# A hybrid decoder layer on one core: in the state-space stage the product is made in place in `yv`, its square goes into the spent `xt` tile, and ScalarE's queue stores it

## The chip, the cores and the metric

The kernel runs on one core of one Trainium2 chip. A core has TensorE (PE in the profile, with its weight loads as PEld), VectorE (DVE), ScalarE (ACT), GpSimd (POOL) and SyncE (SP). Each engine works through its own list of instructions in order; an instruction that has to wait holds up everything behind it on that engine. Transfers between main memory and on-chip memory are issued by an engine's sequencer (SPq, ACTq, POOLq in the profile), on that engine's queue and in that engine's order. The metric is the time of one execution in microseconds (us) on the device; lower is better.

## The reference, cut to what matters

One layer of a decoder trunk with 512 tokens and a width of 1024: RMSNorm, one wide projection `h @ W_in`, three token mixers side by side (top-k attention "DSA", block-sparse attention "NSA", a state-space mixer "SSD"), a gated sum, an output projection, and a feed-forward part. All is float32. The change lies in the end of the state-space mixer:

```python
def ssd_mixer(z, xbc, dt, ...):          # 4 groups x 4 chunks of 128 tokens, 8 heads of 64 per group
    xbc = silu(causal_conv(xbc, conv_w, conv_b))
    ...
    y_diag = einsum('bcijg,bcijgh,bcjgh,bcjghp->bcighp', cb, lmat, dtc, xs)
    states = einsum('bcjgn,bcjgh,bcjghp->bcghpn', bm, decay_states * dtc, xs)
    ...                                   # the state is carried from chunk to chunk
    y_off = einsum('bcign,bcghpn,bcigh->bcighp', cm, h_in, exp(a_cum))
    y = y_diag + y_off + xs * d_skip
    y = rms_norm(y * silu(z), norm_g)     # needs y * silu(z) and the sum of its squares per token
    return y
```

## The kernel before, in words

Two streams of work are interleaved on the engines. The **filler** is the large projections: weights are loaded by SP into `wraw` (3 buffers, L154), split by ScalarE (`whi`, L173) and VectorE (`wlo`, L175) into two parts, and multiplied on TensorE in three passes (L459, L460, L461). The **main** stream is the mixers, stage by stage. A `yield` in the main stream hands over a number of nanoseconds, and the filler is advanced by as much; so the text of the program interleaves both. The framework's scheduler then puts the instructions of each engine in an order of its own, from what waits for what, from the buffers and from priorities; a change in one place can therefore move instructions in the whole of a stage and in those behind it.

The state-space stage has 16 units (group g, chunk c), two groups alternating. Unit i runs through three steps. `stage1` issues the loads of `bcx` (3 buffers) and `E` (3 buffers, 512 KB) on SP. `load_xz` issues the loads of `xs` (2 buffers, L1330) and `xz` (3 buffers, 512 KB, L1332) on SP; half of `xz` is the skip term `u.xd`, the other half the gate `u.zs`. `stage2` masks `E` (POOL, L1345), takes exponentials (ACT: `eab` L1344, `E` L1348), makes `xt` and `xw` on POOL (2 buffers each; L1350, L1353) and multiplies `E` by a small product in bank `pv` (DVE, L1355). `stage3` makes up to two accumulators of tag `sc` (2 banks) and the state update (`hst`, L1374, L1377), eight products per unit of `xt` with `E` on TensorE (L1315), and then the end that the change touches:

- L1384, VectorE: `yv` = product + (`t1`, which lies in `eab`, or the skip term). `yv` has **one** buffer.
- L1395, VectorE: `zs` = `yv` times `zs`, written **into the gate's half of the `xz` tile**.
- L1396, SP: store of that half into `yc_d`, 256 KB. Until it has landed, this buffer of `xz` can't be loaded again.
- L1397, ScalarE: square of `zs` into `yv`.
- L1401, L1403, L1404, POOL: the halves of the square are added, and added to the sums `sq` of that chunk. Until then `yv` can't be written again.

The last two units take another branch (L1386 to L1394): the pool `tl` is open by then, with `zsl` (2 buffers) for the product and `sk` for the sums on VectorE. The outputs `yc_d` are read back much later, in the branch projections (L825).

Of the kernel before, what the change touches and what calls it, by code (L numbers as in the profile page):

```python
# [7 lines left out]
F32 = mybir.dt.float32  # L8
F32R = mybir.dt.float32r
AF = mybir.ActivationFunctionType  # L10
ALU = mybir.AluOpType
# [30 lines left out]
def build_kernel(ctx, tc, A, out):  # L42
    nc = tc.nc
    pe, act, dve, pool = nc.tensor, nc.scalar, nc.vector, nc.gpsimd
# [5 lines left out]
    def bc(ap, shape):  # L50
        return ap.to_broadcast(shape)
# [6 lines left out]
    def popen(name, side="left", space=None, bufs=1):  # L58
        kw = dict(name=name, bufs=bufs, side=side)
        if space is not None:  # L60
            kw["space"] = space
            kw.pop("side")
        cm = tc.tile_pool(**kw)
        p = cm.__enter__()
        open_pools[name] = cm
        return p
# [6 lines left out]
    def scratch(name, shape, dt=F32):  # L73
        return scr_pool.tile(shape, dt, name=name)
# [8 lines left out]
    yc_d = scratch("yc_d", [4, NB, 128, 512])  # L83
# [8 lines left out]
    def ps(tag, shape, dt=F32, bufs=2):  # L92
        if tag == XT[0]:
            XT[1] += 1
            if XT[1] % 3 == 0:
                tag = "pF"
        return psp.tile(shape, dt, tag=tag, name=tag, bufs=PSB[tag])
# [1209 lines left out]
    def ssd(sv, ratio):  # L1307
        sp = popen("ssd", side="right")
# [5 lines left out]
        def mm(*a):  # L1314
            i_ = pe.matmul(*a, start=True, stop=True)  # L1315
            tc.stamp_issue_order_token(getattr(i_, "ins", i_), "ssd")
# [41 lines left out]
        def stage3(u):  # L1358
            g, c = u.g, u.c
            py = ps("sc", [128, 512])  # L1360
            if c:
                po = ps("sc", [128, 512])
                for k in range(4):
                    mm(po[:, 128 * k:128 * k + 128], hst[g][:, 128 * k:128 * k + 128], u.b[:, 1])
                t1 = u.ea.rearrange("p k i -> p (k i)")
                dve.tensor_tensor(t1, po, t1, op=ALU.mult)
                pool.tensor_tensor(t1, t1, u.xd, op=ALU.add)
                yield ratio * 960
            if c < 3:
                pst = ps("pT", [128, 512])  # L1370
                mm(pst, u.b[:, 2], u.xw)
                if c == 0:
                    hst[g] = sp.tile([128, 512], F32, name="hst", bufs=2)
                    act.activation(hst[g], pst, AF.Copy)  # L1374
                else:
                    pool.tensor_tensor(x3(hst[g]), x3(hst[g]), bc(col(sv["dec"], c, g)[:, :, None], [128, 8, 64]), op=ALU.mult)
                    dve.tensor_tensor(hst[g], hst[g], pst, op=ALU.add)  # L1377
                yield ratio * 858
            for h in range(8):
                e, cs = h % 2, slice(128 * (h // 2), 128 * (h // 2) + 128)  # L1380
                mm(py[64 * e:64 * e + 64, cs], u.xt[:, h * 64:h * 64 + 64], u.E[:, h])
            yield ratio * 1300
            yv = (TL[0] or sp).tile([128, 512], F32, name="yv", bufs=1)
            dve.tensor_tensor(yv, py, t1 if c else u.xd, op=ALU.add)  # L1384
            if TL[0] is not None:
                zs = TL[0].tile([128, 512], F32, name="zsl", bufs=2)  # L1386
                dve.tensor_tensor(zs, yv, u.zs, op=ALU.mult)
                nc.sync.dma_start(yc_d[g, c], zs)
                act.activation(yv, zs, AF.Square)
                dve.tensor_tensor(yv[:, 0:256], yv[:, 0:256], yv[:, 256:512], op=ALU.add)  # L1390
                for k in range(2):
                    dve.tensor_tensor(SK[:, c], SK[:, c], yv[:, 128 * k:128 * k + 128], op=ALU.add)
                yield ratio * 100
                return  # L1394
            dve.tensor_tensor(u.zs, yv, u.zs, op=ALU.mult)  # L1395
            nc.sync.dma_start(yc_d[g, c], u.zs)  # L1396
            act.activation(yv, u.zs, AF.Square)  # L1397
            lo, hi = yv[:, 0:256], yv[:, 256:512]
            if sq4[c] is None:
                sq4[c] = sp.tile([128, 256], F32, name=f"sq{c}")  # L1400
                pool.tensor_tensor(sq4[c], lo, hi, op=ALU.add)  # L1401
            else:
                pool.tensor_tensor(lo, lo, hi, op=ALU.add)  # L1403
                pool.tensor_tensor(sq4[c], sq4[c], lo, op=ALU.add)  # L1404
            yield ratio * 100
# [16 lines left out]
        TL, SK = [None], None  # L1422
        for i in range(16):
            if i == 14:
                yield "nq"
                TL[0] = popen("tl")
                SK = TL[0].tile([128, NB, 128], F32, name="sk")
                for c in range(NB):
                    dve.tensor_tensor(SK[:, c], sq4[c][:, 0:128], sq4[c][:, 128:256], op=ALU.add)
            yield from need(i + 2)  # L1430
            if i + 2 < 16:
                load_xz(us[i + 2])
            if i + 1 < 16:
                yield from stage2(us[i + 1])
            yield from stage3(us[i])
# [444 lines left out]
```

## Time and profile before

| | |
|---|---|
| median of 3 runs | 1348.6 us (1346.11 to 1349.12) |
| the profiled execution | 1348.39 us, of which the span of the profile is 1346.7 us |
| PE busy | 1327.0 us, 99% of the span |
| DVE, ACT, POOL busy | 997.3, 728.3, 272.7 us |
| moved by the DMA queues | 213.74 MB, nearly all issued by SP (q1) |
| state-space stage | some 165 us, from the first loads at 405 us to the last product at 566 us |

How to read it: a row of the timeline has its start and its duration in us, the engine, the line, the tiles written and read, and in square brackets how long the engine was idle before it and what ended that. A row of the waits has the engine and the line that waited, what it waited for, the total in us, how often, and the longest. In the table by windows the first column after the stretch is its length, and then the busy time of each engine; "DMA share" is the mean busy share of the 16 DMA engines. Matmuls overlap, so idle time of PE is time in which none was in flight.

### The profile page before, as it was taken

What the parts mean: (1) busy time and instruction counts of PE and PEld (TensorE: products, weight loads), DVE (VectorE), ACT (ScalarE), POOL (GpSimd) and SP (SyncE); (2) the same over time, 40 slices, a digit from 0 to 9 for tenths busy, and PEclk for the clock granted to TensorE, in tenths of its full rate; (3) what the DMA queues carried; (4) which work ended last, traced back from release to release, by engine and by line L of the source; (5) the groups of instructions that cost most, each with busy time, mean ns of one, the idle gap of its engine ahead of it and who ended that gap; (6) DMA issues with size and microseconds to landing.
All of it is one profiled execution on the core that took longest, in us unless ns stands there. A gap on an engine that the chain in (4) does not pass through costs nothing.

```text
span 1346.7 us, 19637 instructions
## 1 busy us (share of the span) xinstructions
PE 1327.0 (99%) x6827; PEld 1107.3 (82%) x6827; DVE 997.3 (74%) x1977; ACT 728.3 (54%) x1395; POOL 272.7 (20%) x238
## 2 busy tenths in 40 slices
PE   9999999999999999999999999999999999999998
PEld 7788888888887767788888888888889888888887
DVE  6489986889977657667688789988654666757841
ACT  5456334777767764656676666565343443444520
POOL 2325111111005669500000022222000201102000
PEclk8999999999999999999999999999999999999999
DMA  6336665455459889653354546343527646746431
GB/s 199 112 91 160 186 180 135 131 158 145 142 160 325 288 283 313 214 175 103 108 155 125 162 133 175 118 149 124 175 78 188 132 151 140 169 124 128 148 121 47
DMA packets 251777, 213.74 MB, mean 159 GB/s; under 512 B 15881, under 2 KB 203165, under 8 KB 251678
## 3 DMA queue, kind: packets, MB, share of 16 engines
q1 hardware_dynamic: 235708, 188.88, 46.4%
q0 software_dynamic: 15232, 20.98, 8.2%
q10 hardware_dynamic: 738, 2.63, 0.6%
q8 instruction: 54, 0.88, 0.3%
q14 instruction: 45, 0.37, 0.1%
HBM read 171.75 MB, written 40.70 MB: 158 GB/s over the span
## 4 chain that ended last, share of the span: by engine, by line
PE 86%; DVE 4%; DMA 4%; POOL 2%; issue 2%; ACT 1%; SPq 0%; DVEq 0%; ACTq 0%; POOLq 0%
PE pj L459 20%; PE pj L461 20%; PE pj L460 20%; PE sc L459 4%; PE sc L460 4%; PE sc L461 3%; PE pT L987 3%; PE pv L999 2%; PE pv L1000 2%; PE sc L928 2%; PE sc L927 2%; PE sc L1315 1%; DMA xs<-x_d 1%; PE pF L987 1%; DMA q_d<-qev 1%
## 5 line engine op out<-in xcount | busy, mean ns | idle before, releaser
L173 ACT ACTIVATE whi<-wraw 128x1024 fp32r<-128x1024 f32 (+2 forms) x190 | 198.3, 1046 | 239.0 <-PE pj L460 117.2
L175 DVE TENSOR_TENSOR wlo<-wraw,whi 128x1024 fp32r<-128x1024 f32 (+1 forms) x176 | 224.7, 1278 | 99.1 <-ACT whi L173 96.4
L459 PE MATMUL pj<-hTh,whi 128*128 128x512 f32 x512 | 203.3, 397 | 3.6 <-DVE cacc L856 2.0
L461 PE MATMUL pj<-hTh,wlo 128*128 128x512 f32 x512 | 202.1, 395 | 0.0
L460 PE MATMUL pj<-hTl,whi 128*128 128x512 f32 x512 | 202.0, 395 | 0.0
L936 ACT ACTIVATE p<-p,nb,rs 128x384 f32<-128x384 f32 (+3 forms) x160 | 107.8, 677 | 37.2 <-DVE nb L934 36.9
L459 PEld LDWEIGHTS pj<-hTh,whi 128*128 128x128 f32 x512 | 96.3, 188 | 22.8 <-ACT eab L1344 2.2
L460 PEld LDWEIGHTS pj<-hTl,whi 128*128 128x128 f32 x512 | 96.3, 188 | 19.1 <-issue 0.7
L461 PEld LDWEIGHTS pj<-hTh,wlo 128*128 128x128 f32 x512 | 96.2, 188 | 19.0 <-issue 0.4
L460 PE MATMUL pj<-h2l,whi 128*128 128x512 f32 (+1 forms) x256 | 96.3, 376 | 0.0
L461 PE MATMUL pj<-h2h,wlo 128*128 128x512 f32 (+1 forms) x256 | 96.2, 376 | 0.0
L459 PE MATMUL pj<-h2h,whi 128*128 128x512 f32 (+1 forms) x256 | 96.1, 376 | 0.0
L459 PE MATMUL pj<-whi,hTh 128*128 128x512 f32 (+2 forms) x208 | 81.3, 391 | 3.0 <-DVE v_s L561 2.2
L460 PE MATMUL pj<-wlo,hTh 128*128 128x512 f32 (+2 forms) x208 | 81.0, 390 | 0.0
L461 PE MATMUL pj<-whi,hTl 128*128 128x512 f32 (+2 forms) x208 | 80.5, 387 | 0.0
L991 ACT ACTIVATE pth<-pT 128x512 fp32r<-128x512 f32 x92 | 53.1, 593 | 48.0 <-PE pT L987 47.5
L1046 POOL DMA_DIRECT2D qu<-q_d x32 | 23.5, 737 | 263.5 <-PE sc L928 175.3
L992 DVE TENSOR_TENSOR ptl<-pT,pth 128x512 fp32r<-128x512 f32 x92 | 61.9, 680 | 5.1 <-ACT pth L991 5.0
L459 PE MATMUL sc<-whi,fh 128*128 128x512 f32 x168 | 65.4, 389 | 0.0
L460 PE MATMUL sc<-wlo,fh 128*128 128x512 f32 x168 | 65.4, 389 | 0.0
L461 PE MATMUL sc<-whi,fo 128*128 128x512 f32 x168 | 65.2, 389 | 0.0
L987 PE MATMUL pT<-ident,p 128*128 128x128 f32 x368 | 60.2, 272 | 0.5 <-DVE p L973 0.5
(431 smaller groups left out, 3281.5 us busy)
## 6 DMA issues: line engine op xcount, KB each, us to landing
wraw<-in_w_in_dram SPq DMA_DIRECT2D x84, 512.0 KB, 4.0
wraw<-in_w_ff_dram SPq DMA_DIRECT2D x58, 512.0 KB, 4.1
qd<-in_w_ff_dram POOLq DMA_DIRECT2D x18, 512.0 KB, 5.8
gld<-g_d SPq DMA_DIRECT2D x35, 256.0 KB, 2.8
q_d<-qev SPq DMA_DIRECT2D x64, 128.0 KB, 4.5
qu<-q_d POOLq DMA_DIRECT2D x32, 256.0 KB, 4.1
E<-ac_d SPq DMA_DIRECT2D x16, 512.0 KB, 6.7
xz<-xzt_d SPq DMA_DIRECT2D x16, 512.0 KB, 5.6
```

The source lines that it names most:

```text
L173: act.activation(hi[:, :m], r[:, :m], AF.Copy)
L175: (pool if i in LOWP else dve).tensor_tensor(lo[:, :m], r[:, :m], f(hi[:, :m]), op=ALU.subtract)
L459: pe.matmul(o, lh, rh, start=first, stop=False)
L460: pe.matmul(o, lh, rl, start=False, stop=False)
L461: pe.matmul(o, ll, rh, start=False, stop=last)
L927: pe.matmul(s_[:, h % w, :n], u.q[h], kh[:, :n], start=True, stop=False)
L928: pe.matmul(s_[:, h % w, :n], u.q[h], kl[:, :n], start=False, stop=True)
L936: act.activation(u.p[h][:, :n], u.p[h][:, :n], AF.Exp, bias=u.nb[:, h:h + 1], scale=rs8[:, u.b, u.h0 + h:u.h0 + h + 1], accum_out=u.sm[:, ...
L987: pe.transpose(pt[:, h], u.p[h][:, kb * 128:kb * 128 + 128], ident)
L991: act.activation(ph, ptf, AF.Copy)
L992: dve.tensor_tensor(pl, ptf, f(ph), op=ALU.subtract)
L999: pe.matmul(o, vk, ph0, start=st, stop=False)
```

## The change

In all units the product is written in place into `yv`. The square goes into `u.xt`, whose data the eight products have read by then (in the last two units into a tile `sqx` of its own, and `yv` has two buffers there). The store is issued by ScalarE, behind the square, and reads `yv`. So a buffer of `xz` is free when the product has been made, `yv` is free when the square and the store have read it, and a buffer of `xt` is free when POOL has added the squares.

```diff
-            yv = (TL[0] or sp).tile([128, 512], F32, name="yv", bufs=1)
+            yv = (TL[0] or sp).tile([128, 512], F32, name="yv", bufs=1 if TL[0] is None else 2)
             dve.tensor_tensor(yv, py, t1 if c else u.xd, op=ALU.add)
+            dve.tensor_tensor(yv, yv, u.zs, op=ALU.mult)
+            s2 = u.xt if TL[0] is None else TL[0].tile([128, 512], F32, name="sqx", bufs=2)
+            act.activation(s2, yv, AF.Square)
+            act.dma_start(yc_d[g, c], yv)
             if TL[0] is not None:
-                zs = TL[0].tile([128, 512], F32, name="zsl", bufs=2)
-                dve.tensor_tensor(zs, yv, u.zs, op=ALU.mult)
-                nc.sync.dma_start(yc_d[g, c], zs)
-                act.activation(yv, zs, AF.Square)
-                dve.tensor_tensor(yv[:, 0:256], yv[:, 0:256], yv[:, 256:512], op=ALU.add)
+                dve.tensor_tensor(s2[:, 0:256], s2[:, 0:256], s2[:, 256:512], op=ALU.add)
                 for k in range(2):
-                    dve.tensor_tensor(SK[:, c], SK[:, c], yv[:, 128 * k:128 * k + 128], op=ALU.add)
+                    dve.tensor_tensor(SK[:, c], SK[:, c], s2[:, 128 * k:128 * k + 128], op=ALU.add)
                 yield ratio * 100
                 return
-            dve.tensor_tensor(u.zs, yv, u.zs, op=ALU.mult)
-            nc.sync.dma_start(yc_d[g, c], u.zs)
-            act.activation(yv, u.zs, AF.Square)
-            lo, hi = yv[:, 0:256], yv[:, 256:512]
+            lo, hi = s2[:, 0:256], s2[:, 256:512]
```

The scheduler's order moves with it, on all engines, from the first unit's end on and through the NSA stage. Three places, around the change from the first pair of groups to the second (about 479 to 505 us of the profile before). First SP, whose list holds the loads of the later units; `q_d` are stores of the query projection. Before:

```order
L1396 DMA yc_d<-xz 128x512
L627 DMA q_d_2_67<-qev 64x512 x4
L1332 DMA xz<-xzt_d 128x2x512
L1323 DMA bcx<-bct_d 128x3x128
L1325 DMA E<-ac_d 128x1024
L1330 DMA xs<-x_d 128x512
```

Now:

```order
L627 DMA q_d_2_67<-qev 64x512 x4
L1332 DMA xz<-xzt_d 128x2x512
L1323 DMA bcx<-bct_d 128x3x128
L1325 DMA E<-ac_d 128x1024
L627 DMA q_d_3_68<-qev 64x512
L1330 DMA xs<-x_d 128x512
```

The store of `yc_d` ahead of them has gone from SP's list; the load of `xz`, with `bcx` and `E` behind it, stands where it stood.

ScalarE, at the same place (`hst` is the copy of a new group's first state). Before:

```order
L622 ACTIVATE qev<-pF 128x512
L1344 ACTIVATE eab<-E 64x512 x2
L1374 ACTIVATE hst<-pT 128x512
L1397 ACTIVATE yv<-xz 128x512
L1348 ACTIVATE E<-E,sv_nac 128x128 x8
```

Now:

```order
L622 ACTIVATE qev<-pF 128x512
L1344 ACTIVATE eab<-E 64x512 x2
L1387 ACTIVATE xt<-yv 128x512
L1388 DMA yc_d<-yv 128x512
L1374 ACTIVATE hst<-pT 128x512
L610 ACTIVATE qraw<-pj 128x512
L612 ACTIVATE sq<-qraw 128x512
L1348 ACTIVATE E<-E,sv_nac 128x128 x8
```

The square is now ahead of `hst`, and the issue of the store stands right behind it; both still stand behind `eab`, which waits for `E`.

VectorE, at the same place. Before:

```order
L1384 TENSOR_TENSOR yv<-sc,eab 128x512
L1355 TENSOR_TENSOR E<-E,pv 128x1024
L1395 TENSOR_TENSOR xz<-yv,xz 128x512
L1384 TENSOR_TENSOR yv<-sc,xz 128x512
L1355 TENSOR_TENSOR E<-E,pv 128x1024
```

Now:

```order
L1384 TENSOR_TENSOR yv<-sc,eab 128x512
L1385 TENSOR_TENSOR yv<-yv,xz 128x512
L1355 TENSOR_TENSOR E<-E,pv 128x1024
L1384 TENSOR_TENSOR yv<-sc,xz 128x512
L614 TENSOR_REDUCE ssn<-sq 128x8
L1385 TENSOR_TENSOR yv<-yv,xz 128x512
L1355 TENSOR_TENSOR E<-E,pv 128x1024
```

The product now follows its sum at once, ahead of the multiplication of `E`; the next sum still has the next unit's `E` behind it.

## The prediction, made before the changed kernel had run

> **What bounds the kernel now.** I read the page first, then PE's idle places along the whole span, then the waits of the other engines in the state-space stage, then the timeline of each engine around the two places where PE stops.
>
> ```profile
> PE 1327.0 (99%) x6827; PEld 1107.3 (82%) x6827; DVE 997.3 (74%) x1977; ACT 728.3 (54%) x1395; POOL 272.7 (20%) x238
> ```
>
> TensorE is the bound: it is without a matmul for 1346.7 - 1327.0 = 19.7 us in all. The change adds no matmul and takes none away, so it is worth what it does to this idle time. By stretches (length, PE, PEld, DVE, ACT, POOL, clock, DMA share, GB/s):
>
> ```profile
> 480.00:500.00 20.00, 17.59 (x115) 13.23 (x115) 9.08 (x13) 11.73 (x29) 9.95 (x11) 1.00 0.84 270
> 500.00:520.00 20.00, 18.89 (x113) 14.63 (x114) 18.37 (x21) 14.15 (x27) 17.98 (x15) 1.00 0.93 299
> 520.00:540.00 20.00, 18.79 (x99) 14.89 (x98) 9.41 (x12) 7.56 (x17) 18.92 (x11) 1.00 1.02 322
> 540.00:560.00 20.00, 18.38 (x116) 14.62 (x115) 12.26 (x16) 14.99 (x37) 14.26 (x13) 1.00 0.67 219
> 700.00:850.00 150.00, 149.16 (x774) 125.19 (x773) 131.84 (x343) 96.66 (x215) 21.16 (x16) 1.00 0.52 150
> 850.00:1000.00 150.00, 149.23 (x804) 126.94 (x803) 116.77 (x244) 75.27 (x143) 23.91 (x17) 1.00 0.43 139
> ```
>
> In the second half of the state-space stage, 480 to 560 us, PE idles 2.41 + 1.11 + 1.21 + 1.62 = 6.35 us of 80; in the 300 us of the attention stage behind it 0.84 + 0.77 = 1.61 us. So a third of all idle time lies in one stage, it lies where the change is, and no gain can be much over 6 us. The places are these (in brackets the idle time and who ended it):
>
> ```profile
> 480.75 0.46 PE L1315 MATMUL pv<-bcx 128*128 128x128 f32 x2 [1.39 <-issue]
> 500.06 0.49 PE L1315 MATMUL pv<-bcx 128*128 128x128 f32 x2 [1.58 <-DVE E L1355]
> 505.89 1.09 PE L1315 MATMUL sc<-E,xt 128*64 128x128 f32 x16 [0.17 <-DVE yv L1384]
> 507.76 0.49 PE L1315 MATMUL pv<-bcx 128*128 128x128 f32 x2 [0.77 <-DVE E L1355]
> 523.33 0.55 PE L619 MATMUL pF<-ident,qraw 128*128 128x128 f32 x3 [1.21 <-DVE qev L623]
> 543.84 0.50 PE L459 MATMUL pj<-hTh,whi 128*128 128x512 f32 x1 [1.62 <-ACT gth L795]
> ```
>
> Three families: 1.58 + 0.17 + 0.77 = 2.52 us behind VectorE, which was late with `yv` and `E`; 1.21 + 1.62 = 2.83 us behind stores of `q_d` and behind ScalarE; 1.39 us for which the profile names no releaser. Who was late behind them:
>
> ```profile
> ACT eab L1344 <- DVE yv L1384: 19.9, 7, 6.6
> ...
> DVE yv L1384 <- POOL sq L1404: 14.4, 5, 8.3
> SPq L1332 <- DMA yc_d<-xz: 21.3, 9, 3.8
> ...
> SPq L1396 <- DVE xz L1395: 10.9, 7, 3.8
> ```
>
> VectorE stood still for 14.4 us because the one buffer of `yv` was still being summed by POOL. SP stood still for 21.3 us because a load of `xz` had to wait for the landing of the store out of the same buffer, and for 10.9 us until there was something to store. Both waits are taken away by the change.
>
> **The change part by part.** *SP gives up 16 stores and the wait for their landing.* The longest stand of VectorE shows what that wait costs (timeline of SP, then of ScalarE, POOL and VectorE):
>
> ```profile
> 479.54 0.33 SPq L1396 DMA_DIRECT2D yc_d<-xz  x1
> 480.30 2.40 SPq L627 DMA_DIRECT2D q_d<-qev  x4
> 485.55 0.36 SPq L1332 DMA_DIRECT2D xz<-xzt_d  x1
> ...
> 486.52 0.44 SPq L1325 DMA_DIRECT2D E<-ac_d  x1
> 493.08 1.27 ACT L1344 ACTIVATE eab<-E 64x512 f32<-64x512 f32 x2 [6.23 <-DMA E<-ac_d]
> 495.00 0.63 ACT L1397 ACTIVATE yv<-xz 128x512 f32<-128x512 f32 x1
> 497.42 0.74 POOL L1404 TENSOR_TENSOR sq<-sq,yv 128x256 f32<-128x256 f32 x1
> 489.22 0.69 DVE L1395 TENSOR_TENSOR xz<-yv,xz 128x512 f32<-128x512 f32 x1
> 498.19 0.69 DVE L1384 TENSOR_TENSOR yv<-sc,xz 128x512 f32<-128x512 f32 x1 [8.29 <-POOL sq L1404]
> ```
>
> SP is done with the stores of `q_d` at 480.30 + 2.40 = 482.70 and issues `xz` at 485.55: 2.85 us lost. `E` stands behind it, lands after 493.08 - 486.52 = 6.56 us, and ScalarE waits for it with the square of `yv` behind. With `xz` free as soon as its product is made, `E` goes out 2.85 us earlier, if its own buffer is free; bounds 0 and 2.85, and I take all of it, since in the rows above nothing else stood between 482.70 and 485.55.
>
> *`yv` is held by a store instead of by POOL.* Then ScalarE starts `eab` at 493.08 - 2.85 = 490.23, the square at 491.50, and it ends at 492.13. The issue of a transfer on ScalarE and the landing have these rows:
>
> ```profile
> 951.48 2.21 ACTq L1632 DMA_DIRECT2D xin<-in_x_dram  x4
> L1396 SPq DMA_DIRECT2D yc_d<-xz x14: 319/333/1781, 425.2 to 554.2; - x14
> ...
> DMA to landing us min/median/max: 3.2/4.7/7.0
> ```
>
> The issue takes 2.21 / 4 = 0.55 us on ScalarE (bounds 0.33 and 1.78 from SP's own stores), the landing 3.2 to 7.0 us, of which I take the median of 4.7, since size and place are the same. So this `yv` would be free at 492.13 + 0.55 + 4.7 = 497.4 where the sum now starts at 498.19: 0.8 us earlier, between 2.3 us earlier and 1.5 us later by the landing alone. Of the 2.52 us that PE lost behind it I take 0.8 as saved, with bounds of 2.3 saved and 1.5 lost.
>
> The rule for the other reuses: now `yv` is free one square and two sums after the product, 0.63 + 2 x 0.74 = 2.1 us; then it is one square, one issue and a landing, 0.63 + 0.55 + 4.7 = 5.9 us. That is 3.8 us more wherever POOL is not late. It is covered as long as the next sum comes later:
>
> ```profile
> L1384 DVE TENSOR_TENSOR yv<-sc,xz x4: 678/688/693, 421.4 to 505.1; 128x512 f32<-128x512 f32 x4
> L1384 DVE TENSOR_TENSOR yv<-sc,eab x12: 676/688/694, 440.7 to 565.2; 128x512 f32<-128x512 f32 x12
> ```
>
> 16 sums from 421.4 to 565.2 us are (565.2 - 421.4) / 15 = 9.6 us apart; less a sum and a product of 0.69 each, 8.2 us are left for a need of 5.9. On the mean the landing fits, by 2.3 us; where units follow closer than 7.3 us it doesn't. What then stands behind the waiting sum on VectorE is the next unit's `E`, `qev` and the splits `wlo`; the order of the changed kernel shows them there.
>
> *Stores of `q_d` and ScalarE at 520 to 544 us.*
>
> ```profile
> 518.22 1.78 SPq L1396 DMA_DIRECT2D yc_d<-xz  x1
> 525.42 0.79 SPq L627 DMA_DIRECT2D q_d<-qev  x1
> 532.20 0.69 DVE L623 TENSOR_TENSOR qev<-pF,qev 128x512 fp32r<-128x512 f32 x1 [4.99 <-DMA q_d<-qev]
> 538.09 1.27 ACT L1344 ACTIVATE eab<-E 64x512 f32<-64x512 f32 x2 [6.65 <-DVE yv L1384]
> ```
>
> VectorE waits 4.99 us for a buffer of `qev`, whose store SP issued at 525.42. One store of `yc_d` ahead of it alone kept SP for 1.78 us. Everything behind, the sum of `yv`, ScalarE's `eab` and the `gth` for which PE waits at 543.84, would come at least 1.78 us earlier, more than the 1.62 us and the 1.21 us that PE lost. The DMA engines' share is 1.02 in this stretch, though, so an earlier issue need not be an earlier landing: bounds 0 and 2.83 saved, and I take 2.4.
>
> The Trainium skill speaks against that part: "DMA: Bandwidth & Descriptors", section "Issuing engines are not separate DMA queues", has it that transfers issued by ScalarE, SyncE and GpSimd run on the same 16 DMA engines and interleave, so that another queue saves only the time of issuing. By it, this term would be 0 and the sum 1347.7. No row here has the same store on two queues; the gain that I count on comes from the wait that SP no longer makes, which that rule does not speak of.
>
> *The rest.* 16 issues on ScalarE are 16 x 0.55 = 8.8 us of an engine that is busy 11.73 + 14.15 + 7.56 + 14.99 = 48.4 of 80 us there; it costs nothing as long as it only follows a square, and up to 1 us of PE where `whi` or `eab` stands behind it. POOL's sums now hold `xt`; they and the next `xt` are on the same engine in the same order as before, so nothing new waits. The 1.39 us at 480.75 stay. In the attention stage the new order has only 1.61 us of idle time to win; I take 0.1 us of loss, bounds 1 us of gain and 4 of loss.
>
> The sum: 1348.4 (profiled execution; 0.2 under the median of 1348.6) - 0.8 - 2.4 + 0.1 = **1345.3 us**.
>
> **The rivals.** *The waits are moved, not removed:* `E` and `q_d` land when the DMA engines have time for them, whoever issues them, and SP's free time turns into a longer time to landing. For it: the DMA share of 0.93 and 1.02 from 500 to 540 us. Against it: 0.84 and 0.67 in the stretches before and behind, in which SP waited. Then the second term is 0, and the first stays: 1348.4 - 0.8 + 0.1 = 1347.7. The same time comes out if the change doesn't do what it says, that is if `xz` is reloaded no earlier because SP now waits at the same place for the product (its wait of 10.9 us is of that kind).
>
> *VectorE behind the store:* the landing takes the place of POOL's sums. It decides where the landing is over 7 us or units are closer than 7.3 us, and the distance from 498.19 to the next sum was under 7. If as many reuses wait as now, five, each 3.8 us longer, VectorE loses 19 us more. Of 14.4 us of such waits PE lost 2.52, a share of 0.175; so 19 x 0.175 = 3.3 us more for PE, and none of the gains: 1348.4 + 3.3 + 0.1 = 1351.8. For it: `yv` keeps one buffer, and ScalarE's square and store stand behind `eab`, which waited 19.9 us. Against it: the mean distance of 9.6 us.
>
> *The attention stage pays:* its order is new from the first unit on, and it idled 1.61 us in 300, less than any other stretch of this kind. At the bound of 4 us of loss, with 1 us of gain left in the state-space stage: 1351.4.
>
> **How the numbers follow.** Forecast 0.44, 1345.3, with a range of its own of 1342 (nearly all 6.35 us gone) to 1345.9; moved waits 0.28; VectorE behind the store 0.18; the attention stage 0.10. About 0.2%, 2.7 us, is what a measurement of this kernel can tell from no change. Forecast is faster, moved waits the same, the last two slower: 0.44, 0.28, 0.28. The range for 8 in 10 reaches from 1341.0 (the bounds of all terms) to 1352.5, over the two slower cases.
>
> **What would show it.** Right: no wait of SP's `xz` for a landing; `yv` waiting for `yc_d` less than 14.4 us in all; PE's gaps near 500 and 543 us under 1 us; `E` issued nearer to the issue of `bcx` with the DMA share at 480 to 500 us above 0.84. Moved waits: the same gaps, with times to landing of `E` above 6.56 us. VectorE behind the store: `DVE yv` waiting for the landing by over 25 us in all, and PE waiting for `E` behind it. The forecast is wrong if PE idles over 6.35 us in the second half of the stage, or over 4 us in the attention stage.

## The result

The change made the kernel slower by about half a per cent, and the time lies outside the predicted range.

| | before | after |
|---|---|---|
| median, four runs each | 1347.57 us (1346.11 to 1349.12) | 1354.91 us (1353.79 to 1355.89) |
| ratio, 95% interval | | 1.0054 [1.0037, 1.0071] |
| measured again (17 and 6 runs) | 1347.26 us | 1354.72 us, ratio 1.0055 [1.0038, 1.0072] |
| span of the profile | 1346.7 us | 1352.4 us |

Forecast were 1345.3 us, with 1341.0 to 1352.5 for 8 in 10. Of the rivals, "VectorE behind the store" (1351.8) is nearest by its time, but it did not happen; "the attention stage pays" (0.10, 1351.4) is nearest by what happened.

The lines of the profile after that answer to those of before are these. First the busy time of the engines, then the windows, in the same columns:

```profile
PE 1329.7 (98%) x6827; PEld 1105.8 (82%) x6827; DVE 994.2 (74%) x1977; ACT 728.7 (54%) x1395; POOL 273.6 (20%) x238
```

```profile
480.00:500.00 20.00, 18.05 (x108) 13.43 (x107) 11.04 (x13) 14.42 (x32) 12.26 (x12) 1.00 0.94 282
500.00:520.00 20.00, 19.69 (x114) 15.37 (x113) 14.79 (x17) 10.23 (x20) 17.98 (x10) 1.00 1.04 330
520.00:540.00 20.00, 17.95 (x98) 14.03 (x97) 12.05 (x13) 10.99 (x25) 18.94 (x15) 1.00 0.77 256
540.00:560.00 20.00, 17.93 (x100) 13.96 (x99) 10.92 (x14) 11.54 (x26) 12.30 (x12) 0.91 0.58 184
700.00:850.00 150.00, 148.66 (x758) 123.32 (x757) 128.86 (x350) 93.79 (x213) 20.01 (x16) 1.00 0.53 150
850.00:1000.00 150.00, 145.14 (x778) 120.95 (x777) 116.37 (x249) 75.30 (x144) 25.82 (x15) 1.00 0.40 130
```

In the second half of the state-space stage PE idles 1.95 + 0.31 + 2.05 + 2.07 = 6.38 us, where it was 6.35: nothing was won. In the attention stage behind it, in which the change has no line, it idles 1.34 + 4.86 = 6.20 us instead of 1.61. These 4.6 us are the larger part of the loss of 7.3. Over the whole span PE idles 1352.4 - 1329.7 = 22.7 us instead of 19.7, since it idles 1.7 us less ahead of 480 us, and it is busy 2.7 us longer; why it is busy longer was not shown.

What the change was to do it did in the main. The waits of SP and of VectorE between 400 and 600 us (total, times, longest):

```profile
SPq L1332 <- DVE yv L1385: 11.5, 5, 5.7
...
SPq L1330 <- POOL xt L1350: 8.0, 4, 2.3
```

```profile
DVE yv L1384 <- DMA yc_d<-yv: 8.1, 3, 5.2
```

SP no longer waits there for the landing of a store (21.3 us before); the load of `xz` now waits 11.5 us for its product (L1385), where before SP also stood 10.9 us ahead of the store. VectorE stands 8.1 us for the landing of the store out of `yv`, where it stood 14.4 us for POOL. But PE's stops went elsewhere (timeline of PE; in brackets the idle time and what ended it):

```profile
486.87 0.33 PE L619 MATMUL pF<-ident,qraw 128*128 128x128 f32 x1 [0.85 <-DVE qev L623]
489.33 0.49 PE L1315 MATMUL pv<-bcx 128*128 128x128 f32 x2 [1.10 <-DVE E L1355]
...
533.25 0.49 PE L1315 MATMUL pv<-bcx 128*128 128x128 f32 x2 [1.89 <-DVE E L1355]
...
555.33 0.50 PE L1439 MATMUL pT<-mhalf,sk 128*128 128x1 f32 x2 [1.92 <-DVE sk L1426]
```

### The profile page after: what moved, and what is told of

The parts are those of the page before. It is cut to its first block, busy times and chain, and to the rows that moved or that the text cites. A ratio compares the mean times of both kernels' runs of the same rounds, so it can differ in the third digit from the quotient of the medians.

```text
span 1352.4 us, 19598 instructions
## 1 busy us (share of the span) xinstructions
PE 1329.7 (98%) x6827; PEld 1105.8 (82%) x6827; DVE 994.2 (74%) x1977; ACT 728.7 (54%) x1395; POOL 273.6 (20%) x238
## 4 chain that ended last, share of the span: by engine, by line
PE 84%; DVE 6%; DMA 5%; issue 2%; ACT 1%; POOL 1%; SPq 0%; ACTq 0%; DVEq 0%; POOLq 0%
PE pj L459 20%; PE pj L460 20%; PE pj L461 19%; PE sc L461 3%; PE sc L460 3%; PE sc L459 3%; PE pT L987 3%; PE pv L1000 2%; PE pv L999 2%; PE sc L928 2%; PE sc L927 2%; DMA gld<-g_d 1%; PE sc L1315 1%; DVE wlo L175 1%; DMA q_d<-qev 1%
## 5 line engine op out<-in xcount | busy, mean ns | idle before, releaser
L175 DVE TENSOR_TENSOR wlo<-wraw,whi 128x1024 fp32r<-128x1024 f32 (+1 forms) x176 | 221.7, 1261 | 103.7 <-ACT whi L173 100.9
```

What stands on the lines that cost most here:

```text
L175: (pool if i in LOWP else dve).tensor_tensor(lo[:, :m], r[:, :m], f(hi[:, :m]), op=ALU.subtract)
```

## The loss in the attention stage: one stop in detail

In the attention stage every instruction is the same as before; only its place in each engine's list differs, from the first state-space unit to the end of the branch projections. One of the stops shows what that does. The timeline of PE, ScalarE and VectorE after:

```profile
955.33 0.40 PE L1000 MATMUL pv<-ptl,v_s 128*128 128x512 f32 x1
955.56 0.28 PE L459 MATMUL pj<-yhB,whi 128*128 128x256 f32 x1
...
956.16 0.28 PE L461 MATMUL pj<-yhB,wlo 128*128 128x256 f32 x1
957.74 0.51 PE L459 MATMUL pj<-yhB,whi 128*128 128x256 f32 x2 [1.30 <-ACT yhB L1011]
```

```profile
955.76 0.59 ACT L1005 ACTIVATE yt<-pv 64x512 f32<-64x512 f32 x1 [2.60 <-PE pv L1000]
957.27 0.42 ACT L1011 ACTIVATE yhB<-yr 128x256 fp32r<-128x256 f32 x1 [0.91 <-DVE yr L1010]
```

```profile
956.39 0.85 DVE L1010 TENSOR_TENSOR yr<-pv,yt 64x256 f32<-64x256 f32 x2 [0.94 <-ACT yt L1005]
```

The last attention unit ends with `pv` at 955.33. From it ScalarE makes `yt`, VectorE `yr`, ScalarE `yhB`, one after the other: 957.27 + 0.42 - 955.76 = 1.9 us. Between that `pv` and the first matmul that reads this `yhB` the list has six other matmuls, from 955.56 to 956.16: some 0.7 us of cover. PE stands for 1.30 us. The same place in the profile before (PE, then ScalarE):

```profile
948.76 0.40 PE L1000 MATMUL pv<-ptl,v_s 128*128 128x512 f32 x1
949.00 0.28 PE L459 MATMUL pj<-yhB,whi 128*128 128x256 f32 x1
...
951.87 0.28 PE L461 MATMUL pj<-yhB,wlo 128*128 128x256 f32 x1
951.99 0.40 PE L459 MATMUL pj<-yhB,whi 128*128 128x256 f32 x2
```

```profile
949.20 0.60 ACT L1005 ACTIVATE yt<-pv 64x512 f32<-64x512 f32 x1 [3.92 <-PE pv L1000]
950.71 0.42 ACT L1011 ACTIVATE yhB<-yr 128x256 fp32r<-128x256 f32 x1 [0.91 <-DVE yr L1010]
```

There the chain takes the same 950.71 + 0.42 - 949.20 = 1.9 us, 951.99 - 949.00 = 3.0 us of matmuls cover it, and PE doesn't stop. The other large stops of this stage (1.22 us before `sc` at 872.47, 0.88 us before `pj` at 905.67) are waits for VectorE (`mx`, `gld`); their chains were not followed.

## The experiments

To part the order from what the change does on the chip, an order was written into a kernel as a table: the instructions of each engine in the wished sequence, each tied to the one before it by an edge that only fixes who is issued first and adds no wait (shortened; in the kernel the table is packed).

```diff
+    for e, t in table.items():
+        seq = [ins[e][k] for k in t]
+        for x, y in zip(seq, seq[1:]):
+            tc.add_manual_dep(y, x.name, NO_SYNC, reason="order of the other kernel")
```

Theory O is that the order makes the loss, theory C that something carried over from the state-space stage does.

**The kernel before, with the attention stage in the new order.** Table: the list of the changed kernel from the last state-space unit on.

> The kernel before, unchanged in what it computes and in its order up to the last state-space unit, and from there on in the order of the changed kernel. Theory O: this alone makes the loss, 1352 to 1356 us, ratio 1.003 to 1.007, with the attention stage idle for about 6 us. Theory C: 1346 to 1349, ratio within 0.1% of 1.

1353.80 us, ratio 1.0040 [1.0027, 1.0052]. The windows:

```profile
700.00:850.00 150.00, 148.43 (x756) 122.94 (x755) 128.46 (x347) 93.13 (x212) 20.01 (x16) 1.00 0.53 149
850.00:1000.00 150.00, 145.70 (x784) 122.19 (x783) 116.35 (x246) 75.75 (x145) 25.82 (x15) 1.00 0.41 129
```

No line of the kernel before was touched, and it idles 1.57 + 4.30 = 5.87 us there and loses 5.4 us (0.40% of 1348; 3.6 to 7.0). Its largest stops stand at the places of the changed kernel, before the same matmuls (timeline of PE):

```profile
871.09 0.45 PE L927 MATMUL sc<-kh_j,qu 128*128 128x384 f32 x1 [1.31 <-DVE mx L929]
...
903.62 0.50 PE L459 MATMUL pj<-yhA,whi 128*128 128x512 f32 x1 [0.83 <-DVE gld L1609]
...
955.68 0.50 PE L459 MATMUL pj<-yhB,whi 128*128 128x256 f32 x2 [1.30 <-ACT yhB L1011]
```

So the order alone makes this loss, without anything carried over: theory O holds. Whether something carried over adds to it, the next runs ask.

**The changed kernel, with the attention stage in the old order.** Table: the list of before, once from the last unit on, and once from some 20 us later.

> The changed kernel, its own order of instructions up to the last state-space unit, and from there to the end the order of the kernel before, on all five engines. Theory O (the loss is the new order of the attention stage, and nothing that the change does on the chip): the attention stage idles about 1.6 us again instead of 6.2 and its matmuls follow each other as before; time 1346 to 1349.5 us, ratio to the kernel before 0.999 to 1.0015. Theory C (something carried over from the state-space stage, such as later loads, stores that are still under way or buffers that come free later, slows the attention stage): the loss stays, 1353 to 1356, ratio 1.004 to 1.006.

> The changed kernel in its own order to some 20 us behind the last state-space unit, and from there to the end in the order of the kernel before, so that the seam between the two orders lies in work that only depends on the attention stage itself. Theory O with additive stages: 1347 to 1350. Theory S (the state-space stage costs about as much as the whole loss, and the attention stage's idle time adds little to it): 1352 to 1356, as with the earlier seam.

The early seam gave 1354.26 us, ratio 1.0047 [1.0030, 1.0064], the late one 1349.31, ratio 1.0022 [1.0011, 1.0032]. The late one, windows:

```profile
700.00:850.00 150.00, 149.31 (x773) 125.33 (x772) 132.74 (x340) 95.20 (x208) 21.68 (x16) 1.00 0.52 148
850.00:1000.00 150.00, 149.09 (x804) 127.04 (x803) 115.58 (x243) 75.31 (x143) 23.43 (x16) 1.00 0.44 137
```

The idle time is back at 0.69 + 0.91 = 1.60 us. Beside the changed kernel measured with it (below) that is 0.33% or 4.4 us by the ratios, 1354.72 - 1349.31 = 5.4 us by the medians. So theory C falls for the late seam: the stage's loss goes. Neither expectation held in full, since the kernel stays 3.0 us (0.22%) behind. The early seam idles as little in the attention stage (1.86 us) and shows next to none of the gain in its time, against theory O; all that differs is 88 matmuls behind the seam and their partners on the other engines. In its profile the granted clock was 0.83 in two stretches of 10 us (from 490 and from 560 us) instead of one, and PE idles 7.1 us from 480 to 560 us instead of 5.4. The two intervals just overlap; why the early seam lost so much was not found.

**The changed kernel again.**

> The changed kernel itself, for a second profile and a time on the same chip and beside the same runs of the kernel before as the runs of this call: 1353 to 1357, ratio 1.0037 to 1.0071 as measured; idle time of 700 to 1000 us 5.5 to 7 us. The state-space stage (from the first state-space matmul to the last) took 157.5 us in the first profile against 155.8 before; if its loss is real, it takes over 157 again.

1354.72 us, ratio 1.0055 [1.0038, 1.0072]; PE idles 1.42 + 4.21 = 5.63 us from 700 to 1000 us. From 480 to 560 us it idles only 4.69 us here, where the first profile had 6.38. The kernel before shows the same spread in a second execution (e2, whose order is its own up to the last unit): 4.68 us and 6.35. So in this stretch the two kernels differ by nothing that shows, and two executions of one kernel by 1.7 us. The state-space stage took 156.2 us from its first matmul to its last, so this count of the first profile (157.5 against 155.8) was no measure of its loss.

**Each layout in the other's order, from start to end.** Does an order suit the layout that it was not made for? In the first of the two runs POOL's list is left to the scheduler: in the order of before, POOL would wait for sums that stand behind in its own list.

> The changed kernel (product in yv, square in xt, store on ScalarE's queue) in the order of the kernel before on PE, DVE, ACT and SP from start to end; each store stands right behind its square; POOL's order is left to the scheduler, since the kernel before makes the next xt ahead of the sums that now hold it. Theory O: the attention stage is that of the kernel before; what the change does on the chip shows alone, in the state-space stage: by the prediction's terms 3.2 us gained, by its rival of moved waits 0.8; so 1344 to 1348, ratio 0.9975 to 1.0005. Theory C: 1353 or more.

> The kernel before (product in xz, square in yv, store on SP) in the order of the changed kernel on all five engines from start to end. Theory O: at least the loss of the attention stage, 1353 to 1358, ratio 1.004 to 1.008; the waits of the old buffers come on top where the new order was not made for them. Theory C: 1346 to 1350.

1407.03 us, ratio 1.0429 [1.0411, 1.0448], and 1374.31 us, ratio 1.0191 [1.0172, 1.0209]. Both missed by far, and the waits of SP between 400 and 640 us, and between 400 and 600 us, say why. The change in the order of before:

```profile
SPq L1330 <- POOL xt L1350: 98.1, 12, 17.9
```

The kernel before in the order of the change:

```profile
SPq L1332 <- DMA yc_d<-xz: 50.2, 12, 6.0
```

In the first, a tile of `xt` is held until POOL has added the squares, the next `xt` waits for that, the load of `xs` waits for the next `xt`, and SP stands at it for 98.1 us with everything else behind. `xt` has two buffers, so the next tile in the same buffer is that of two units later. In the profile before, POOL makes all 14 such tiles ahead of the sums of the unit two before; in that of the change it makes them behind (two neighbouring rows of POOL's list, before and after):

```
L1350 TENSOR_TENSOR xt<-xs,sv_dth 128x512
L1404 TENSOR_TENSOR sq_4087<-sq_4087,yv 128x256

L1401 TENSOR_TENSOR sq_4087<-sq_4087,xt 128x256
L1350 TENSOR_TENSOR xt<-xs,sv_dth 128x512
```

So in the order that was there on the other four engines the changed kernel takes 59 us more, and the hold on `xt` is its largest wait; the other parts of the change were in this run too. That the new order is the scheduler's answer to the hold is likely, but not shown. In the change's own order SP waits at that load for 8.0 us, against 6.9 before.

**The parts of the change, one at a time.** Only the store moved to ScalarE (likewise in the last two units):

```diff
             dve.tensor_tensor(u.zs, yv, u.zs, op=ALU.mult)
-            nc.sync.dma_start(yc_d[g, c], u.zs)
             act.activation(yv, u.zs, AF.Square)
+            act.dma_start(yc_d[g, c], u.zs)
```

> The kernel before with one part of the change: the product stays in the z half of the xz tile and the square in yv, and only the store of the product is issued by ScalarE, behind the square, instead of by SP. The scheduler gives nearly the order of the kernel before (17 of 6574 matmuls stand elsewhere). Theory O (the loss is the new order of the attention stage): that stage keeps its idle time of 1.6 to 2 us, and what is left is the queue's own effect, 0 to 2 us either way: 1346 to 1350 us, ratio 0.9985 to 1.0015. Rival Q (the store on ScalarE's queue costs by itself, through 16 issues of 0.35 us between ScalarE's instructions and the later landing): 1350 to 1355, ratio over 1.002.

1353.39 us, ratio 1.0040 [1.0025, 1.0055]: what rival Q expected, with the order of the matmuls nearly that of before. SP's waits from 400 to 600 us:

```profile
SPq L1332 <- DMA yc_d<-xz: 31.4, 7, 6.8
```

The store is issued behind the square, so it lands later, and here the load of `xz` still waits for the landing: 31.4 us instead of 21.3. But the attention stage idles 3.50 us, not the 1.6 to 2 that theory O gave it, and PE idles 1.7 us more than before from 400 to 480 us; how much of the loss the wait makes was not parted from that.

Only the square moved into `xt` (product, store and queue as before):

```diff
-            act.activation(yv, u.zs, AF.Square)
-            lo, hi = yv[:, 0:256], yv[:, 256:512]
+            s2 = u.xt
+            act.activation(s2, u.zs, AF.Square)
+            lo, hi = s2[:, 0:256], s2[:, 256:512]
```

> The kernel before with one part of the change: the square goes into the spent xt tile, product in the z half and store by SP as before; the last two units are as before. yv is free once the product is made. The next xt waits for POOL's sums. Its order of the attention stage is a fourth one. Theory O: the state-space stage is within 3 us of before, and the attention stage by its order idles 1.5 to 7 us: 1346 to 1356. Rival H (the hold on xt costs the state-space stage itself, through SP's load of xs that waits for xt's product): SP waits over 20 us for POOL at that load, and PE idles over 9 us between 480 and 580 us.

1353.46 us, ratio 1.0043 [1.0027, 1.0059]. SP waits 10.8 us for `xt`, not over 20, so rival H has no support; the attention stage idles 1.91 + 1.67 = 3.58 us from 700 to 1000 us, 2.0 more than before and a third of the loss; a good part of the rest lies at 560 to 580 us, where the first matmuls of the attention stage stop 2.9 us for transfers and the granted clock is 0.80 and 0.86 in two stretches of 10 us.

The change with the store back on SP:

```diff
-            act.dma_start(yc_d[g, c], yv)
+            nc.sync.dma_start(yc_d[g, c], yv)
```

> The changed kernel with one part undone: the product in yv and the square in xt as in the change, but the store issued by SP again. The scheduler gives it a third order of the attention stage, unlike that of either kernel. Theory O: the time goes by that order, so the idle time of 700 to 1000 us says it all: 1.5 to 7 us, and the time is that of the kernel before plus the idle time over 1.6 us, 1347 to 1356. Rival Q: the loss goes away with the queue whatever the order, 1346 to 1349.

1349.75 us, ratio 1.0015 [0.9999, 1.0031], with 1.81 + 1.38 = 3.19 us of idle time in 700 to 1000 us. As theory O has it, the order of this program decides, though by this run alone it could be the queue.

The change with the square in the z half instead of in `xt` (all but the last two units; shortened):

```diff
-            act.activation(s2, yv, AF.Square)
+            act.activation(u.zs, yv, AF.Square)
             act.dma_start(yc_d[g, c], yv)
-            lo, hi = s2[:, 0:256], s2[:, 256:512]
+            lo, hi = u.zs[:, 0:256], u.zs[:, 256:512]
```

> The changed kernel with one part altered: the square goes into the spent z half of the xz tile instead of into xt; product in yv and store by ScalarE out of yv as in the change. xt is free after the matmuls again, and the attention stage comes out in nearly the order of the kernel before (7 of its 2057 matmuls stand elsewhere). Theory O: the attention stage idles 1.6 to 2 us and the state-space stage shows the change's own worth, between 3 us gained and 2 us lost: 1345 to 1350, ratio 0.998 to 1.0015. Rival X (the product in yv with the landing of its store ahead of the next sum is what costs): 1351 to 1356, with VectorE's yv waiting over 15 us for the landing.

1347.49 us, ratio 1.0004 [0.9988, 1.0020]: level with the kernel before. VectorE waits only 4.5 us for the landing of the store, so rival X falls, and product in `yv` and store on ScalarE's queue are not what costs. With where the square stands, the attention stage also came out in nearly the old order. Its idle time is 3.05 us all the same, not the 1.6 to 2 expected: 1.79 of it is one stop for `pth` (ScalarE), which was 0.21 us before. The next two runs part place and order. Table: the list of the changed kernel, once from the last unit on, once from start to end.

> The same kernel with the square in the z half, in its own order up to the last state-space unit, and from there on in the order of the changed kernel. Its own order gave a ratio of 1.0004. Theory O with the loss in the attention stage: 1352 to 1356, ratio 1.003 to 1.006, as when the kernel before was given this order. Theory S (the loss sits in the state-space stage, and the two orders of the attention stage are worth the same once that stage is good): 1346 to 1349.5, ratio under 1.0015.

> The kernel with the square in the z half of xz (product in yv, store by ScalarE), which took as long as the kernel before in its own order, now in the order of the changed kernel on all five engines from start to end. Beside the changed kernel it differs in one thing alone: xt is free after the matmuls, and the z half is held until POOL's sums. Theory O (the order makes the loss): 1352 to 1357 us, ratio 1.003 to 1.007, with 5 to 6.5 us of idle time between 700 and 1000 us. Theory X (the hold on xt makes the loss, by what it does on the chip): 1345 to 1350, ratio within 0.2% of 1.

With the attention stage of the changed kernel: 1352.83 us, ratio 1.0036 [1.0023, 1.0050], so the new order costs 0.32% (4.3 us) a third time; it idles 5.56 us. With the changed kernel's order throughout: 1370.81 us, ratio 1.0176 [1.0159, 1.0193], missed by both theories. SP's waits there:

```profile
SPq L1332 <- POOL sq L1404: 27.1, 9, 8.1
```

The z half is held by POOL's sums now, and the list calls for `xz` too early for that. A third time an order written for another layout does badly.

**The rest of 3 us.** In the changed kernel's list POOL has four operations `rs` (powers) of the attention stage ahead of work for the next state-space units (timelines of POOL after, and of VectorE):

```profile
510.84 13.13 POOL L1809 TENSOR_TENSOR rs<-ssn,mhalf 128x16 f32<-128x16 f32 x4
523.94 1.04 POOL L1376 TENSOR_TENSOR hst<-hst,sv_dec 128x512 f32<-128x512 f32 x1
...
530.19 2.08 POOL L1345 TENSOR_SCALAR_AFFINE_SELECT E<-E 128x1024 f32<-128x1024 f32 x1
```

```profile
525.02 0.69 DVE L1377 TENSOR_TENSOR hst<-hst,pT 128x512 f32<-128x512 f32 x1 [6.66 <-POOL hst L1376]
```

VectorE stands 6.66 us for `hst`, `E` is late, and PE stops for 1.89 us at 533.25. In the profile before, `hst` and the first select stand ahead of the block. Theory P: this block, and the fall of the clock behind such stops, is the rest. The four alone were moved back behind `hst`, the sum into `eab` and the first select, as in the profile before, with every other order kept (the list of POOL). It is one select of `E`, for which the list has two entries; the next one stays behind the block:

```diff
 xt<-xs,sv_dth
-rs<-ssn,mhalf x4
 hst<-hst,sv_dec
 eab<-eab,xz
 E<-E
+rs<-ssn,mhalf x4
```

So it was done in the changed kernel, and in the one with the old attention stage; the block went further back, behind the sum into `eab` of the next unit, in the kernel with the square in the z half and in the kernel before.

> The changed kernel in its own order on PE, DVE, ACT and SP, and on POOL too but for one block: the four products rs (13 us together), which the change put ahead of hst, the sum into eab and two selects of E, stand behind these again, as in the kernel before. Theory P (this block makes the rest of the loss, 3 us, by a late E and the fall of the clock after it): no idle time over 1 us near 535 us, the granted clock 1.00 throughout the state-space stage, 1350 to 1352.5 us, ratio 1.002 to 1.004, the rest being the order of the attention stage. Theory X (the hold on xt makes it): still 1353 to 1356.

> The changed kernel with the attention stage in the order of the kernel before (late seam, ratio 1.0022 without more), and the four products rs moved behind hst, eab and the two selects as well. Theory P: both losses are gone, 1345 to 1348.5 us, ratio 0.9985 to 1.0008. Theory X: 1348.5 to 1351, ratio 1.001 to 1.003.

> The kernel with the square in the z half (ratio 1.0004 in its own order) in that order, with the four products rs on POOL moved some way further back, behind hst, eab and the next unit's work. Its idle times of 1.98 and 1.26 us at 543 and 548 us both wait for E. By theory P they shrink and the kernel comes out ahead of both kernels: 1343 to 1346.5 us, ratio 0.997 to 0.9995. If E is late there for another reason: 1346.5 to 1349.

> The kernel before in its own order, with the four products rs on POOL moved behind the next unit's sums, as a control: its idle times in the state-space stage end on other releasers than E at this place, so theory P gives it little: 1345 to 1349, ratio 0.998 to 1.001. Over 1.002 would say that the products are wanted early by something, and the gain of the other runs of this call would have a price.

Ratios 1.0070 [1.0047, 1.0094], 1.0027 [1.0011, 1.0042], 0.9990 [0.9975, 1.0005] and 1.0056 [1.0037, 1.0075]. Theory P falls. In the first run its signs came: no stop over 1 us near 535 us, and a granted clock of 1.00 from 480 to 560 us. But the stop became several (timeline of PE), and nothing was gained.

```profile
533.88 0.49 PE L1315 MATMUL pv<-bcx 128*128 128x128 f32 x2 [0.41 <-DVE E L1355]
538.28 0.50 PE L459 MATMUL pj<-hTh,whi 128*128 128x512 f32 x1 [0.70 <-ACT gth L795]
540.32 0.49 PE L1315 MATMUL pv<-bcx 128*128 128x128 f32 x2 [0.61 <-DVE E L1355]
556.50 0.38 PE L1439 MATMUL pT<-mhalf,sk 128*128 128x1 f32 x2 [1.42 <-DVE sk L1426]
```

In the kernel before, moving the block cost 0.56%. What stays is that the rest goes with the square in `xt`: with the old attention stage, the change is at 1.0022 and 1.0027, both intervals above 1; with the square in the z half it is at 1.0004 and 0.9990, both intervals around 1. By which wait was not shown. Since layout and list differ together in the state-space stage, it may be the hold on `xt` or again the order that answers it.

**What the new order of the attention stage costs, pair by pair.** In each row the two kernels differ in this list alone; in the last row the list called old is only nearly that of before. The figures are the ratio to the kernel before and PE's idle time from 700 to 1000 us.

| the rest of the kernel | old list | new list |
|---|---|---|
| before | 1; 1.61 us | 1.0040; 5.87 us |
| changed (old list from the late seam on) | 1.0022; 1.60 us | 1.0055; 5.63 us |
| changed, `rs` moved | 1.0027; 1.53 us | 1.0070; 6.29 us |
| square in the z half | 1.0004; 3.05 us | 1.0036; 5.56 us |

The steps are 0.40, 0.33, 0.43 and 0.32%, or 4.3 to 5.8 us, each uncertain by some 0.2%. The early seam, with a step of 0.07%, is the one that does not fit.

**The queue alone, and the best variant again.** The kernel with the square in the z half and the moved block, a second time, and with its store on SP in the same order:

```diff
-            act.dma_start(yc_d[g, c], yv)
+            nc.sync.dma_start(yc_d[g, c], yv)
```

> The kernel with the square in the z half and the four products rs moved back, a second time. It was 0.999 of the kernel before, interval 0.9975 to 1.0005. If the gain is real (its state-space stage idled 4.4 us against 9.0 before): 1343 to 1346.5, ratio 0.9975 to 0.9998 again. If it was chance: 1.000 to 1.0015.

> The kernel of run g1 in the same order on all engines, but for the store of the product out of yv, which SP issues instead of ScalarE; SP's other transfers stay in their order. Theory Q1 (the queue is of no weight by itself, since the store leaves out of yv and no load waits for its landing): within 0.15% of run g1. Theory Q2 (ScalarE's issues cost, as the run with only the store moved seemed to say): 1 to 5 us faster than g1. Theory Q3 (SP's queue in front of the store is what ScalarE's queue saves): 1 to 5 us slower than g1, SP waiting at the store for the product by 5 us or more.

1.0000 [0.9986, 1.0015] and 0.9992 [0.9982, 1.0003]. The queue is of no weight where no load waits for the landing, as theory Q1 has it, and no variant was shown to be ahead of the kernel before. These kernels are written as a table from start to end and are level with it, so the table shows no cost of its own.

In these runs the gain in the state-space stage did come: with the square in the z half and the block moved, PE idles 2.3 to 2.6 us from 480 to 560 us (three profiles), against 6.35 and 4.68 in the kernel before. The attention stage gives much of it back, with 3.4, 3.4 and 5.4 us of idle time instead of 1.6. This layout with the attention stage in the list of before was not run.

## Why the prediction was wrong

*The step that failed* is the last term: "In the attention stage the new order has only 1.61 us of idle time to win; I take 0.1 us of loss, bounds 1 us of gain and 4 of loss." It measured 5.4 us (3.6 to 7.0) in the kernel before, 4.4 in the changed kernel with the late seam, 5.8 in that with `rs` moved and 4.3 in the variant with the square in the z half. The term was named and had a rival of its own, but its bound was too small, and its middle was put at nearly nothing though the profile showed what it was made of: a stage that idles 1.61 us in 300 has its covers already laid, so a new order can hardly win and can lose each of them. The way of the loss, stops of PE where less work covers a chain, was not in the text, which gave the new order no sum; the middle was a guess.

*"Nothing new waits" for `xt`* was wrong. The text said that POOL's sums and the next `xt` stand "in the same order as before". In the list of before the next `xt` of the same buffer is ahead of the sums, 14 times of 14. With the other engines in that order the changed kernel takes 59 us more, and it is in the variants with the square in `xt` that the rest of 3 us stays. The order on POOL was there to be read.

*The two gains of 0.8 and 2.4 us* did not come, though the waits they rested on went. The stops at 500, 506 and 508 us and those at 523 and 544 us are gone, and as large ones stand at 487, 489, 533 and 555 us: 6.38 us for 6.35, and in a second execution of each 4.69 for 4.68. That is the rival "the waits are moved", but further than it said: not to longer landings (`E` 6.9 us at the median against 6.7, `yc_d` 5.4 against 5.1) but to other instructions. The 2.4 us had no sum behind them: between the store of `yc_d` at 518.22 and that of `q_d` at 525.42 SP also issued seven other transfers, so 1.78 us less for the one need not bring the other forward by as much. The 0.8 us took the landing from a view that holds the last two units' stores as well; the 14 stores of L1396 alone have a median of 5.1 us, by which it would have been 0.4. "VectorE behind the store" did not happen: 8.1 us of waiting for the landing, where 25 were asked for.

*The range* began at 1341.0 "(the bounds of all terms)", but these bounds give 1348.4 - 2.3 - 2.83 - 1 = 1342.3. At the other end the bounds of loss were not added up: 1.5, 0, 4 and the 1 us for the issues on ScalarE come to 1354.9, beyond the 1352.5 that was given. That this sum is the time measured is chance, since the first and the last of the four were not what was lost.

*The signs* named for its being right came: no wait of `xz` for the landing of a store, `yv` at 8.1 us, stops under 1 us near 500 and 543 us, a DMA share of 0.94 from 480 to 500 us. So did both that were to prove it wrong: 6.38 us over 6.35 (within what two executions differ by), and 6.20 over 4. The signs of a mechanism do not tell whether it pays.

*On the rule that was weighed against the second term:* the Trainium skill, "DMA: Bandwidth & Descriptors", section "Issuing engines are not separate DMA queues", has another queue save the time of issuing only. Runs g1 and g2 agree within their intervals: 1.0000 [0.9986, 1.0015] and 0.9992 [0.9982, 1.0003] for the same store on ScalarE's queue and on SP's.

The sum as the runs have it, by the ratios of one set of runs (the changed kernel again, and with the late seam): 4.4 us for the new order of the attention stage and 3.0 us that go with the square in `xt`, 7.4 against 7.3 measured. For product and store on ScalarE's queue nothing was found (1.0004 with the square in the z half). The first term is shown; how the second comes about stays open.

## What to carry to other kernels

Where a scheduler lays out the whole program, an edit in one stage is also a new draw for every stage behind it, and a stage that hardly idles has little to win by it and more to lose: give that term a middle on the losing side, and test it by writing the old order into the new kernel, and the new into the old. Before a tile is used twice, look up in the list of its next writer whether that write stood ahead of the last reader; if it did, the hold is new, whatever the engine. And an order of a stage does badly with other buffers than those it was made for: three crossings of the state-space stage cost 24 to 59 us.

## What the runs showed of the hardware

The granted clock fell in short stretches in which PE stopped, or right behind them, and by the estimate below a fall costs about as much as the stop. Windows of 10 us in the second profile of the changed kernel, and in the variant with the square in the z half:

```profile
530.00:540.00 10.00, 7.63 (x41) 5.18 (x40) 7.10 (x7) 8.85 (x22) 9.59 (x8) 0.83 0.64 179
```

```profile
540.00:550.00 10.00, 6.76 (x51) 4.79 (x50) 5.84 (x7) 6.90 (x18) 5.85 (x6) 1.00 0.80 245
```

As an estimate, 0.83 over 10 us are 0.17 x 10 = 1.7 us of matmul time lost, beside the stop of 2.37 us in that stretch; it shows as busy time. The second kernel stood longer in its 10 us (3.24 us, in two stops of 1.98 and 1.26) and its clock did not fall; in the first profile of the changed kernel it fell around a stop of 1.92 us at 555 us and not around one of 1.89 us at 533 us. The plainest case lies ahead of every line that the change touches: a stop of 2.2 us that ends between 65 and 68 us is in each of the 20 profiles, and from 60 to 70 us the clock was 0.83 to 0.89 in 8 of them and 1.00 in 12. So a stop of some 2 us may or may not bring a fall. The Trainium skill, "TensorE: Matmul & The Clock Gate", section "HAM oscillation — how this bites in real kernels", warns of stops over some 3.4 us; the falls here came with shorter ones, and by the measurement the warning begins too late.

The same program in two executions (g1, and f3 before it, on another chip) shows the size of it: spans of 1348.0 and 1341.5 us, idle times of 17.1 and 16.5 us, mean granted clocks of 0.993 and 0.999. So two executions of one program can differ by 6 us with nearly the same idle time, almost as much as the change cost; single profiles are therefore no measure of it, and the ratios above rest on 4 to 12 runs of a kernel.
